# Per-layer gate: all four pairs' weight sums made by transfers, e's first half read back behind the pairs

## The chip, the cores and the metric

The kernel runs on one core of a Trainium2 chip. The metric is the device time of one execution in microseconds (us). The core's engines are TensorE (PE, with its weight loads PEld), VectorE (DVE), ScalarE (ACT), GpSimd (POOL) and SyncE (SP). Here SP issues nearly all transfers, and POOL issues only the transfers that add to what they find.

## The reference

One decoder layer over 256 tokens of width 2048: a mixer of two attention branches, a feed-forward part with a causal convolution, and a per-layer embedding with a gate. The change is in the last part, of which this is the whole:

```python
h = h + rmsnorm(f, g_ffn_post[i])
e = p[i] @ w_ple_in[i]                       # (256, 256) @ (256, 2048)
h = h + jax.nn.sigmoid((h @ w_ple_gate[i]).astype(jnp.float32)).astype(h.dtype) * e
```

All is float32. `w_ple_gate` is 2048 x 2048, so `h @ w_ple_gate` has 16 blocks of 128 along the sum (k) and 16 columns of 128.

## The kernel before

**Items.** All weights lie packed in one tensor `w`, in the order in which PE uses them, as items of 128 x 1024 floats (eight 128 x 128 blocks). An item is loaded into a tile `raw` (a ring of NRAW = 5), by `load` on SP. ScalarE copies it to `hi` in a rounded format (function `high`, L238, or L234 for sums), and VectorE subtracts to get the rest, `lo` (function `low`, L301, or L295 for sums). `hi` and `lo` are rings of NSPL = 7. A product is three matmuls (`three_wide`, L945): hi by hi, lo by hi, hi by lo. `lows` makes the `lo` of items up to a number, and then issues the raw loads for which a `raw` tile has come free. `tick` is called at each new item: it first calls deferred ScalarE jobs, then `high` for the items ahead, `lows`, and deferred VectorE jobs. Every engine works its instructions in the order in which this code writes them.

**Gate stage.** It has 40 items. Items 0 to 7 are columns 0 to 3 (two k blocks in each; loop over `k`, 16 steps). Items 8 to 13 are k = 8 to 13 of columns 4 to 11, eight blocks each. Items 14 to 29 are four "pairs" of k blocks, (0,1), (2,3), (4,5), (6,7), of the same columns, which are multiplied by a Strassen scheme (`strassen`): it needs seven products (21 matmuls) instead of eight. Items 30 and 31 are k = 14 and 15, and items 32 to 39 are columns 12 to 15 (`four`): t = 0 and t = 1 are the two halves of the tokens, and from k = 10 on t = 0 is finished first, then t = 1, the end of it in two parts.

**Pairs.** Each pair has four items: two raw ones with weights (14, 18, 22, 26 full; 17, 21, 25, 29 of which half is split) and between them two items of sums of weights. `weight_sums` makes them on VectorE: the first item by two additions (L254, L255), the second from the first by two more (L257, L258). For pairs in `by_dma` the first item is made by transfers instead: `sum_to` (L271) loads one summand with a plain transfer on SP, and `add_to_sums` (L277) has POOL issue two transfers with `accum_op=OP.add` that add the other summand, and then L254 and L255 fall away and the second raw item of the pair is loaded by half. `DSUM` says for how many pairs: five in each quarter of the feed-forward part, two in the gate. `sum_early` issues them ahead, into tiles that are free there (`tsum`).

The other factor of a pair, sums of columns of `h`, is made by `parts`: four small additions on VectorE, a copy on ScalarE, a subtraction on VectorE into `mixed` (L1209 to L1218). The list `made[n]` holds these three steps of mixture n.

**e.** Half of e (columns 0 to 1023) is computed early, and written to a tensor `e0` in HBM. The other half is computed at the start of the gate stage and kept in the tile `ee` (128 x 2 x 2048: t, columns), columns 1024 to 2047 of each t. Its first half is read back in two transfers inside the loop over k (L1559, at n = 5 and 6, where n = k // 2 + 1 at odd k).

**End.** `finish` multiplies the gate by `ee`, adds `hx` (h) and writes out. Column 0 to 511 of both t's come first, then 512 to 1535 of each t after a sigmoid, then 1536 to 2047, t = 1 in two halves.

Of the kernel before, what the change touches and what calls it, by code (L numbers as in the profile page):

```python
# [8 lines left out]
F32 = mybir.dt.float32  # L9
# [6 lines left out]
D = 2048  # L16
KT = D // 128
# [16 lines left out]

PAIRS = 4
DROWS = 10
DSUM = {"down": DROWS // 2, "pg": 2}
SETTLE = dict(even=8, turned=9)

TURNED = {("qk", s, 1): 3 for s in (2, 3)}  # L40
# [100 lines left out]
def hybrid_block_kernel(ctx: ExitStack, tc: tile.TileContext, head, gx, pT, convp, bias, masks, gains, w, out):  # L141
    nc = tc.nc
# [11 lines left out]
    def scope(name, **kw):  # L154
        st = ExitStack()
        return st, st.enter_context(tc.tile_pool(name=name, bufs=1, reuse_waits="tile", **kw))
# [6 lines left out]
    for g in _plan():  # L163
        if g[0] == "pad":
            short.append(used // 8)
        if _pairs(g):
# [4 lines left out]
            for p in range(_pairs(g)):  # L171
                i, r = len(stream), len(stream) - 2 * len(sums_of)
                stream += [r, None, None, r + 1]
                sums_of[i] = i + 3
                if g[0][0] == "pairs" and p < DSUM[g[0][1]]:
                    early_sums.append(i)
# [51 lines left out]
    def high(i, a=0, b=1024, src=None):  # L228
        if i not in hi:
            hi[i] = wsp.tile([128, 1024], F32R, name="hi")  # L230
            lo[i] = wsp.tile([128, 1024], F32R, name="lo")
        if i in sums:
            for n, x in enumerate(weight_sums(i)):
                ACT.activation(hi[i][:, n * 512:(n + 1) * 512], x, AF.Copy)  # L234
            return
        if i in part:
            b = 512
        ACT.activation(hi[i][:, a:b], raw[i][:, a:b] if src is None else src, AF.Copy)  # L238
# [30 lines left out]
    def sum_to(i, to):  # L269

        nc.sync.dma_start(to, w[stream[i] - NE])  # L271
        add_to_sums(i, [to[:, :512], to[:, 512:]])

    def add_to_sums(i, to):

        for x in to:
            nc.gpsimd.dma_start(x, w[stream[i] + 1 - NE][:, 512:], accum_op=OP.add)  # L277
        raw[i + 1] = to

    def sum_early(n):  # L280

        i = early_sums.pop(0)
        if n != 1:
            sum_to(i, mps["mp"].tile([128, 1024], F32, name="tsum", tag=f"hx{n - 1}" if n else "tsum"))
            return
        to = [tmp.tile([128, 512], F32, name="tsum", tag="t", bufs=2) for _ in range(2)]
        for c, x in enumerate(to):
            nc.sync.dma_start(x, w[stream[i] - NE][:, c * 512:(c + 1) * 512])
        add_to_sums(i, to)
# [13 lines left out]
    waiting, jobs, mps = [], [], {}  # L303

    def defer(*stages):


        waiting.append(list(stages))
# [8 lines left out]
    def lows(upto):  # L317

        while at["low"] < min(upto, at["cap"]):
            low(at["low"])  # L320
            at["low"] += 1
        while at["load"] in place and at["load"] < gone[at["low"]] + NRAW:
            load(place[at["load"]])
            at["load"] += 1

    def tick(i):


        now = due()
        for act, _ in now:  # L330
            act and act()
        before = at["high"]
        upto = -1 if at["hold"] else reach(i)
        at["look"] = min(at["look"] + at["grow"], NSPL - 1)
        while at["high"] <= upto:
            high(at["high"])
            at["high"] += 1
        late = len(waiting) > 2
        for _, dve in now:
            late and dve and dve()  # L340
        if not at["hold"]:
            lows(max(before, min(i + 2, at["high"])))
        for _, dve in now:
            late or dve and dve()
# [9 lines left out]
    def block(n=1):  # L354

        b = at["block"]
        at["block"] = b + n
        i, c = divmod(b, 8)
        if c == 0:
            tick(i)  # L360
        return hi[i][:, c * 128:(c + n) * 128], lo[i][:, c * 128:(c + n) * 128]
# [642 lines left out]
    for j in range(0, KT, 4):  # L1004
        if j:
            ga, gb = gate_groups(j, merged)
        else:
            for kind in ("ga", "gb"):
# [3 lines left out]
                if kind == "ga":  # L1012
# [7 lines left out]
                    mg_sc, mp = scope("mp")  # L1020
# [81 lines left out]
    def cut(src, k, t):  # L1102
        return [src[:, k, i * T + t * H:i * T + (t + 1) * H] for i in range(2)]
# [73 lines left out]
    def residual():  # L1177
        return [fp.tile([128, 2, 512], F32, name="hx", tag=f"hx{n}") for n in range(4)]

    hx = residual()  # L1180
# [5 lines left out]
    e0 = dram.tile([128, 2, D // 2], F32, name="e0")  # L1186
# [11 lines left out]
    def mixing(ps):  # L1198
        x = keep.tile([128, PAIRS, 2, 4, H], F32R, name="mixed", tag="gh")
        for p in range(ps):  # L1200
            mixed[p] = x[:, p] if p < PAIRS else fp.tile([128, 2, 4, H], F32R, name="mixed4", tag="hx0")
# [108 lines left out]
    def join(o, bk):  # L1310

        tt = DVE.tensor_tensor
        tt(o[1, 0], bk[7], o[0, 1], OP.add)
        tt(o[1, 1], bk[5], o[1, 0], OP.subtract)
        tt(o[0, 1], bk[5], o[0, 1], OP.subtract)
# [74 lines left out]
    def weigh(t, n):  # L1390
        o = ff[:, t, n * 512:(n + 1) * 512]
        DVE.tensor_tensor(o, o, g3[:, n * 512:(n + 1) * 512], OP.mult)
# [7 lines left out]
    for q in range(NQ):  # L1400
# [35 lines left out]
        def reload(n):  # L1436
            nc.sync.dma_start(hx[n], h1[:, :, n * 512:(n + 1) * 512])
# [25 lines left out]
        if end:  # L1463
            hx = residual()
# [14 lines left out]
    def apply(a, b, ts=range(2)):  # L1479

        for t in ts:
            x = hx[a // 512][:, t, a % 512:a % 512 + b - a]
            DVE.scalar_tensor_tensor(x, ff[:, t, a:b], rs[:, t], x, op0=OP.mult, op1=OP.add)
# [4 lines left out]
    for t in range(2):  # L1488
        to = ff[:, t, 3 * 512:]
# [10 lines left out]
    ee = fp.tile([128, 2 * D + 3 * 512], F32, name="ee", tag="ft")  # L1500
    xs = [ee[:, 2 * D + n * 512:2 * D + (n + 1) * 512] for n in range(3)]
    xs.append(fp.tile([128, 512], F32, name="xs", tag="cpad"))
    ee = ee[:, :2 * D].rearrange("p (t c) -> p t c", t=2)
# [3 lines left out]
    def turn_back(n):  # L1507
        turned[n] = bank()
        for k in range(2):
            for t in range(2):  # L1510
                a = (2 * n + k) % 4 * 128
                PE.transpose(turned[n][:, k * T + t * H:k * T + (t + 1) * H], hx[n // 2][:, t, a:a + 128], idf)

    def high3(n):
        x, to = turned[n].rearrange("p (a b) -> p a b", a=2), u3[:, 2 * n:2 * n + 2]
        ACT.activation(to[:, :, :T], x, AF.Copy)

    def save3(n):
        n < PAIRS and ACT.activation(xs[n], turned[n], AF.Copy)

    def low3(n):
        x, to = turned[n].rearrange("p (a b) -> p a b", a=2), u3[:, 2 * n:2 * n + 2]
        DVE.tensor_tensor(to[:, :, T:], x, f(to[:, :, :T]), OP.subtract)  # L1523

    def mixture(n):
        return parts(n, xs[n][:, :T], xs[n][:, T:])

    def ahead():
        lows(at["high"])
        high(at["high"])  # L1530
        at["high"] += 1
# [8 lines left out]
    def keep_e(n):  # L1540
        c, t = divmod(n, 2)
        ACT.activation(ee[:, t, D // 2 + c * 512:D // 2 + (c + 1) * 512], pse[n], AF.Copy)
# [8 lines left out]
    made = []  # L1551
    for k in range(KT):
        if k % 2 and k < KT - 1:
            n = k // 2 + 1
            turn_back(n)
            high3(n)
            low3(n)
            n == 1 and reload(3)
            n in (5, 6) and nc.sync.dma_start(ee[:, :, (n - 5) * 512:(n - 4) * 512], e0[:, :, (n - 5) * 512:(n - 4) * 512])  # L1559
            save3(n)  # L1560
            n < 4 and keep_e(n)
            n < 7 and apply(256 * n + 256, 256 * n + 512)
            n < 3 and [weigh(t, n + 1) for t in range(2)]
            n == 6 and [stage() for stage in made[0][1:]]
            if n == KT // 2 - 1:
                made.append(mixture(1))
                [stage() for stage in made[1]]
            n <= DSUM["pg"] and sum_early(n - 1)
        if k == 8:
            mixing(PAIRS)  # L1570
        if k == 10:
            made.append(mixture(0))
            made[0][0]()
        if k % 2 and k < KT - 2:
            ahead()
        w2 = block(4)
        for t in range(2):
            three_wide(ps[t], cut(u3, k, t), w2, k == 0, k == KT - 1)
    at["hold"], at["look"], at["grow"] = False, 2, 1
    ACT.preload_act_table(AF.Sigmoid)  # L1580
    def finish(spans):

        for t, a, b in spans:
            o = ff[:, t, a:b]
            DVE.tensor_tensor(o, o, ee[:, t, a:b], OP.mult)
            for c in range(a, b, 512):
                x = min(b - c, 512)
                to = ff[:, t, c:c + x]
                DVE.tensor_tensor(to, to, hx[c // 512][:, t, c % 512:c % 512 + x], OP.add)
            nc.sync.dma_start(out[:, t, a:b], o)  # L1590
# [12 lines left out]
    bk = next(s)  # L1603
    join_first(o, bk)
    defer((None, lambda bk=bk, o=o: join(o, bk)))
    next(s)
    defer((None, lambda bk=bk, o=o: ends(o, bk)))
    defer((None, lambda: finish([(t, 0, 512) for t in range(2)])))
    for t in range(2):
        defer((lambda t=t: ACT.activation(ff[:, t, 512:1536], ff[:, t, 512:1536], AF.Sigmoid),  # L1610
               lambda t=t: finish([(t, 512, 1536)])))
    ps = [bank() for _ in range(2)]
    four(("pg", 12), ps, u3, by=6, split=4)
    flush()
# [78 lines left out]
```

## Time and profile before

| | us |
|---|---|
| median of 3 executions | 1428.39 (1427.77 to 1428.44) |
| the profiled execution, its time | 1427.80 |
| the profiled execution, its span | 1426.0 |
| TensorE busy | 1418.9 |
| VectorE busy | 1174.4 |
| ScalarE busy | 866.9 |
| gate stage in the span | about 1329 to the end |

Times in views are microseconds from the span's start. A line of a timeline gives the start, the length, the engine, the line of the kernel, the instruction, what it writes and reads with the shapes, and how many are merged; in brackets the idle time of the engine before it and what ended that. SPq and POOLq are the queues that issue transfers. A matmul's length overlaps the next one's, so the distance between starts is its cost. The granted clock of TensorE was 0.999.

### The profile page before, as it was taken

Reading aid. Unit: us, or ns where it says so; the run is one execution under the profiler, and the core shown is the slowest. Engines: PE = TensorE matmul, PEld = TensorE weight load, DVE = VectorE, ACT = ScalarE, POOL = GpSimd, SP = SyncE. Lnnn points to the kernel's source line nnn. Section 1 sums busy time; section 2 is a strip of 40 time slices with the busy share of each in tenths; the row PEclk is TensorE's granted clock in tenths of the full one; section 3 lists DMA queues with packets and bytes.
Section 4 is the critical chain, followed back from the end, with each engine's and each line's share of the span. In section 5 each row is a group of like instructions: output and inputs, shape, how many; then the busy total and the mean of one; then the engine's idle time right before and its main releaser. Section 6 shows DMA issues by size and latency. Waiting matters only on the chain.

```text
span 1426.0 us, 20698 instructions
## 1 busy us (share of the span) xinstructions
PE 1418.9 (100%) x7499; PEld 1219.8 (86%) x7499; DVE 1174.4 (82%) x1821; ACT 866.9 (61%) x1316; POOL 60.5 (4%) x73
## 2 busy tenths in 40 slices
PE   9999999999999999999999999999999999999998
PEld 8888888888888888898888888888888888888886
DVE  7876666569889865689999788997889978899798
ACT  7665555566655655576666656655566555666564
POOL 0000000002110000000000000000000000000000
PEclk9999999999999999999999999999999999999999
DMA  7754746469986766648876886377873778628754
GB/s 293 268 165 156 248 146 222 150 237 250 303 229 201 264 219 215 201 168 265 256 204 209 266 265 213 103 262 237 267 214 100 263 236 267 214 99 289 247 186 163
DMA packets 95959, 312.26 MB, mean 219 GB/s; under 512 B 10480, under 2 KB 11120, under 8 KB 95728
## 3 DMA queue, kind: packets, MB, share of 16 engines
q1 hardware_dynamic: 86064, 293.10, 60.6%
q0 software_dynamic: 9792, 17.83, 7.4%
q8 instruction: 59, 0.97, 0.3%
q14 instruction: 44, 0.36, 0.1%
HBM read 305.64 MB, written 5.24 MB: 218 GB/s over the span
## 4 chain that ended last, share of the span: by engine, by line
PE 98%; DVE 2%; ACT 0%; issue 0%; ACTq 0%
PE mm L382 33%; PE mm L945 29%; PE mm L384 17%; PE mm L708 2%; PE mm L710 2%; PE mm L709 2%; PE mm L863 2%; PE mm L864 2%; PE mm L865 2%; PE S L382 0%; DVE lo L301 0%; PE mm L404 0%; PE mm L403 0%; PE mm L402 0%; PE S L721 0%; PE po L721 0%
## 5 line engine op out<-in xcount | busy, mean ns | idle before, releaser
L301 DVE TENSOR_TENSOR lo<-raw,hi 128x1024 fp32r<-128x1024 f32 (+1 forms) x498 | 579.1, 1180 | 96.1 <-ACT hi L238 91.4
L382 PE MATMUL mm<-u,hi 128*128 128x512 f32 x1804 | 627.8, 392 | 0.0
L238 ACT ACTIVATE hi<-raw 128x1024 fp32r<-128x1024 f32 (+1 forms) x498 | 502.1, 1022 | 173.3 <-PE mm L382 54.5
L384 PE MATMUL mm<-u,lo 128*128 128x256 f32 x1791 | 501.5, 280 | 0.0
L382 PEld LDWEIGHTS mm<-u,hi 128*128 128x128 f32 x1804 | 336.7, 187 | 72.7
L384 PEld LDWEIGHTS mm<-u,lo 128*128 128x128 f32 x1791 | 338.5, 189 | 0.7
L945 PE MATMUL mm<-hi,ft 128*128 128x512 f32 x504 | 162.6, 389 | 0.0
L945 PE MATMUL mm<-hi,u 128*128 128x512 f32 (+1 forms) x464 | 147.9, 389 | 0.2
L440 ACT ACTIVATE t<-mm 128x256 f32<-128x256 f32 x131 | 49.7, 380 | 149.3 <-PE mm L384 149.3
L945 PEld LDWEIGHTS mm<-hi,ft 128*128 128x128 f32 x504 | 94.6, 188 | 20.0 <-DVE ff L1308 0.4
L945 PEld LDWEIGHTS mm<-hi,u 128*128 128x128 f32 x464 | 86.4, 188 | 18.5 <-DVE u L1523 0.9
L945 PE MATMUL mm<-lo,ft 128*128 128x512 f32 x252 | 98.5, 391 | 0.0
L443 DVE TENSOR_TENSOR s<-mm,t 128x256 f32<-128x256 f32 x116 | 48.9, 422 | 51.9 <-ACT t L440 51.9
L945 PE MATMUL mm<-lo,u 128*128 128x512 f32 (+1 forms) x232 | 89.8, 387 | 0.8 <-DVE lo L301 0.6
L382 PE MATMUL mm<-mg,hi 128*128 128x512 f32 x232 | 80.5, 392 | 0.0
L277 POOL DMA_DIRECT2D tsum<-in_w x44 | 38.8, 1022 | 881.2 <-DMA tsum<-in_w 309.7
L234 ACT ACTIVATE hi<-wsum 128x512 fp32r<-128x512 f32 x76 | 46.2, 629 | 42.6 <-DVE wsum L257 30.2
L945 PE MATMUL mm<-hi,mixed 128*128 128x512 f32 x192 | 67.0, 389 | 0.0
L384 PE MATMUL mm<-mg,lo 128*128 128x256 f32 x230 | 64.4, 280 | 0.0
L1232 ACT ACTIVATE cv<-cpad,cw 128x256 f32<-128x256 f32 x88 | 52.5, 596 | 12.0 <-DVE cpad L1227 11.9
L945 PEld LDWEIGHTS mm<-lo,ft 128*128 128x128 f32 x252 | 47.3, 188 | 10.6 <-DVE lo L295 1.1
L945 PEld LDWEIGHTS mm<-lo,u 128*128 128x128 f32 x232 | 43.6, 188 | 10.2 <-DVE lo L301 1.2
(327 smaller groups left out, 1913.8 us busy)
## 6 DMA issues: line engine op xcount, KB each, us to landing
raw<-in_w SPq DMA_DIRECT2D x466, 512.0 KB, 4.3
tsum<-in_w POOLq DMA_DIRECT2D x44, 256.0 KB, 7.1
raw<-in_w SPq DMA_DIRECT2D x36, 256.0 KB, 2.9
tsum<-in_w SPq DMA_DIRECT2D x17, 512.0 KB, 4.4
gh<-in_w SPq DMA_DIRECT2D x12, 512.0 KB, 5.5
gh<-in_w POOLq DMA_DIRECT2D x24, 256.0 KB, 7.4
hd<-in_head SPq DMA_DIRECT2D x6, 576.0 KB, 7.3
gh<-in_gx SPq DMA_DIRECT2D x6, 512.0 KB, 4.4
```

What stands on the lines that cost most here:

```text
L234: ACT.activation(hi[i][:, n * 512:(n + 1) * 512], x, AF.Copy)
L238: ACT.activation(hi[i][:, a:b], raw[i][:, a:b] if src is None else src, AF.Copy)
L277: nc.gpsimd.dma_start(x, w[stream[i] + 1 - NE][:, 512:], accum_op=OP.add)
L301: DVE.tensor_tensor(lo[i][:, a:b], raw[i][:, a:b] if src is None else src, f(hi[i][:, a:b]), OP.subtract)
L382: PE.matmul(ps, wh, rhs, start=first, stop=last, skip_group_check=True)
L384: PE.matmul(ps[:, :T], wl, rhs[:, :T], start=False, stop=last, skip_group_check=True)
L440: ACT.activation(t1[0], ps[:, T:], AF.Copy)
L443: DVE.tensor_tensor(out, ps[:, :T], t1[0], OP.add)
L708: PE.matmul(pv[t], xh, wh, start=kt == 0, stop=False)
L709: PE.matmul(pv[t], xh, wl, start=False, stop=False)
L945: PE.matmul(ps, x[i], w[j], start=first and n == 0, stop=last and n == 2, skip_group_check=True)
L1232: ACT.activation(y, c[:, 2:], AF.Identity, scale=cw[:, n, 2:3], bias=cw[:, n, 3:4])
```

## The change

`DSUM["pg"]` goes from 2 to 4, so that the first item of sums of pairs three and four is also made by transfers. Their place is the first half of `ee` (128 x 1024 for each of t = 0 and 1), at n = 4 and 5 of the loop. The readback of e's first half leaves the loop and is issued, one transfer for each t, after the first part of the Strassen product, behind all raw loads. `mixture(1)` is split: its four additions stay, its copy and subtraction come after `ahead()`, the next item's `lo` and `hi`. At the end `finish` for columns 0 to 511 is done for each t for itself, beside the sigmoids.

```diff
-DSUM = {"down": DROWS // 2, "pg": 2}
+DSUM = {"down": DROWS // 2, "pg": PAIRS}
...
-    def sum_early(n):
+    def sum_early(n, to=None):
 
         i = early_sums.pop(0)
+        if to is not None:
+            sum_to(i, to)
+        elif n != 1:
+            sum_to(i, mps["mp"].tile([128, 1024], F32, name="tsum", tag=f"hx{n - 1}" if n else "tsum"))
         if n != 1:
-            sum_to(i, mps["mp"].tile([128, 1024], F32, name="tsum", tag=f"hx{n - 1}" if n else "tsum"))
             return
...
-            n in (5, 6) and nc.sync.dma_start(ee[:, :, (n - 5) * 512:(n - 4) * 512], e0[:, :, (n - 5) * 512:(n - 4) * 512])
...
                 made.append(mixture(1))
-                [stage() for stage in made[1]]
-            n <= DSUM["pg"] and sum_early(n - 1)
+                made[1][0]()
+            n <= 2 and sum_early(n - 1)
+            n in (4, 5) and sum_early(n - 2, ee[:, n - 4, :D // 2])
...
         if k % 2 and k < KT - 2:
             ahead()
+        k == KT - 3 and [stage() for stage in made[1][1:]]
...
     defer((None, lambda bk=bk, o=o: join(o, bk)))
+    for t in range(2):
+        nc.sync.dma_start(ee[:, t, :D // 2], e0[:, t])
     next(s)
     defer((None, lambda bk=bk, o=o: ends(o, bk)))
-    defer((None, lambda: finish([(t, 0, 512) for t in range(2)])))
     for t in range(2):
         defer((lambda t=t: ACT.activation(ff[:, t, 512:1536], ff[:, t, 512:1536], AF.Sigmoid),
-               lambda t=t: finish([(t, 512, 1536)])))
+               lambda t=t: finish([(t, 0, 512)])))
+        defer((None, lambda t=t: finish([(t, 512, 1536)])))
```

PE's instructions are the same, in the same order. In the changed kernel line numbers behind `sum_early` are 3 to 6 higher.

VectorE at the end of items 0 to 7, where mixture 1 is made (`y` are its four additions, `mixed` its subtraction, `lo<-raw,hi` the items' rest). Before:

```order
L1210 TENSOR_TENSOR y_13357<-y_13357,ee 128x128
L1211 TENSOR_TENSOR y_13357<-ee 128x128
L1212 TENSOR_TENSOR y_13357<-y_13357,ee 128x128
L1218 TENSOR_TENSOR mixed<-y_13357,mixed 128x512
L301 TENSOR_TENSOR lo<-raw,hi 128x1024 x3
```

After:

```order
L1213 TENSOR_TENSOR y_13361<-y_13361,ee 128x128
L1214 TENSOR_TENSOR y_13361<-ee 128x128
L1215 TENSOR_TENSOR y_13361<-y_13361,ee 128x128
L304 TENSOR_TENSOR lo<-raw,hi 128x1024
L1221 TENSOR_TENSOR mixed<-y_13361,mixed 128x512
L304 TENSOR_TENSOR lo<-raw,hi 128x1024 x2
```

The `lo` of item 8 has moved ahead of `mixed`; those of items 9 and 10 stay behind it.

VectorE in pair three (pair four reads the same), from the second raw item of pair two on. Before:

```order
L301 TENSOR_TENSOR lo<-raw,hi 128x512
L254 TENSOR_TENSOR wsum<-raw 128x512
L255 TENSOR_TENSOR wsum<-raw 128x512
L301 TENSOR_TENSOR lo<-raw,hi 128x1024
L295 TENSOR_TENSOR lo<-wsum,hi 128x512 x2
L257 TENSOR_TENSOR wsum<-wsum,raw 128x512
L258 TENSOR_TENSOR wsum<-wsum,raw 128x512
L295 TENSOR_TENSOR lo<-wsum,hi 128x512 x2
```

After:

```order
L304 TENSOR_TENSOR lo<-raw,hi 128x512
L304 TENSOR_TENSOR lo<-raw,hi 128x1024
L257 TENSOR_TENSOR wsum<-ee,raw 128x512
L258 TENSOR_TENSOR wsum<-wsum,raw 128x512
L298 TENSOR_TENSOR lo<-ee,hi 128x512 x2
L298 TENSOR_TENSOR lo<-wsum,hi 128x512 x2
```

L254 and L255 are gone, and the additions of the second item (L257, L258) now stand ahead of the `lo` of the first, which reads `ee`.

VectorE at the end, from the last four additions of the Strassen part on (L1338 before, L1341 after; `lo` are items 37 to 39, `ff<-ff,ee` the product of `finish`). Before:

```order
L1338 TENSOR_TENSOR ff<-ff,mm 128x512 x4
L301 TENSOR_TENSOR lo<-raw,hi 128x1024 x2
L1585 TENSOR_TENSOR ff<-ff,ee 128x512
L1589 TENSOR_TENSOR ff<-ff,hx 128x512
L1585 TENSOR_TENSOR ff<-ff,ee 128x512
L1589 TENSOR_TENSOR ff<-ff,hx 128x512
L301 TENSOR_TENSOR lo<-raw,hi 128x1024
L1585 TENSOR_TENSOR ff<-ff,ee 128x1024
```

After:

```order
L1341 TENSOR_TENSOR ff<-ff,mm 128x512 x4
L304 TENSOR_TENSOR lo<-raw,hi 128x1024
L1589 TENSOR_TENSOR ff<-ff,ee 128x512
L1593 TENSOR_TENSOR ff<-ff,hx 128x512
L304 TENSOR_TENSOR lo<-raw,hi 128x1024 x2
L1589 TENSOR_TENSOR ff<-ff,ee 128x1024
```

The first product with `ee` now stands ahead of the `lo` of items 38 and 39, and the second one's t = 1 behind them. On SP the two transfers into `ee` now stand behind the last raw load and ahead of the first output; on ScalarE the first of the two sigmoids stands ahead of the `hi` of item 39.

## Prediction

> **What bounds the kernel now.** I read the page first, for the engine whose work is the end, and then the waits of that engine alone.
>
> ```profile
> span 1426.0 us, 20698 instructions
> PE 1418.9 (100%) x7499; PEld 1219.8 (86%) x7499; DVE 1174.4 (82%) x1821; ACT 866.9 (61%) x1316; POOL 60.5 (4%) x73
> ...
> PE 98%; DVE 2%; ACT 0%; issue 0%; ACTq 0%
> ```
>
> ```profile
> PE z L594 <- DVE epsb L563: 1.1, 1, 1.1
> PE mm L945 <- DVE lo L301: 0.6, 1, 0.6
> PE mm L945 <- DVE lo L295: 0.2, 1, 0.2
> ```
>
> TensorE is the bound: 98% of the chain is matmuls, and in the whole span PE waited three times by the table of waits. The first wait is the start. The other two, 0.6 and 0.2 us, both lie in the gate stage that is changed, and both wait for a `lo` written by VectorE. The change leaves PE's instructions alone, in kind and order, so it can give back only what PE loses in those places, and can take away only by making a new wait. The table counts too little, since a matmul also loses time while its weights wait, so I read PE's timeline by the distance from start to start (columns: start, us, instruction, in brackets the idle time before it).
>
> ```profile
> 1340.36 0.43 PE L945 MATMUL mm<-lo,u 128*128 128x512 f32 x1
> 1340.90 0.73 PE L945 MATMUL mm<-hi,u 128*128 128x512 f32 x2
> ...
> 1355.39 0.61 PE L945 MATMUL mm<-hi,u 128*128 128x512 f32 x2
> 1355.84 0.39 PE L945 MATMUL mm<-lo,u 128*128 128x512 f32 x1
> 1356.07 0.61 PE L945 MATMUL mm<-hi,u 128*128 128x512 f32 x2
> 1357.26 0.50 PE L945 MATMUL mm<-lo,u 128*128 128x512 f32 x1 [0.57 <-DVE lo L301]
> 1357.59 0.63 PE L945 MATMUL mm<-hi,u 128*128 128x512 f32 x2
> ...
> 1390.03 0.39 PE L945 MATMUL mm<-lo,mixed 128*128 128x512 f32 x1
> 1390.26 0.39 PE L945 MATMUL mm<-hi,mixed 128*128 128x512 f32 x1
> 1390.77 0.49 PE L945 MATMUL mm<-hi,u 128*128 128x512 f32 x1
> 1391.50 0.50 PE L945 MATMUL mm<-lo,u 128*128 128x512 f32 x1 [0.23 <-DVE lo L295]
> 1391.83 0.39 PE L945 MATMUL mm<-hi,u 128*128 128x512 f32 x1
> ```
>
> In stride a matmul follows the last by 0.23 us (1390.03 to 1390.26), and two of them by 0.45 (1355.39 to 1355.84). Stall A: after 1356.07 the next but one was due at 1356.52 and came at 1357.26, 0.74 late; the one behind it lost 0.10 more (0.33 for 0.23). A is 0.84 us. Stall B: 0.51, 0.73 and 0.33 us in place of 0.23, so 0.28 + 0.50 + 0.10 = 0.88 us. A third loss, at 1340.90 (0.54 for 0.23, 0.31 us, and about 0.1 in the next), waits for a `u` that the change does not touch. Whose lateness makes A and B is seen on DVE.
>
> ```profile
> 1350.59 1.04 ACT L238 ACTIVATE hi<-raw 128x1024 fp32r<-128x1024 f32 x1
> ...
> 1354.39 0.28 DVE L1212 TENSOR_TENSOR y<-y,ee 128x128 f32<-128x128 f32 x1
> 1355.38 0.69 DVE L1218 TENSOR_TENSOR mixed<-y,mixed 128x512 fp32r<-128x512 f32 x1 [0.70 <-ACT mixed L1215]
> 1355.98 2.35 DVE L301 TENSOR_TENSOR lo<-raw,hi 128x1024 fp32r<-128x1024 f32 x2
> 1359.67 1.23 DVE L301 TENSOR_TENSOR lo<-raw,hi 128x1024 fp32r<-128x1024 f32 x1 [1.33 <-ACT hi L238]
> ...
> 1378.24 0.68 DVE L254 TENSOR_TENSOR wsum<-raw 128x512 f32<-128x512 f32 x1
> 1378.84 0.68 DVE L255 TENSOR_TENSOR wsum<-raw 128x512 f32<-128x512 f32 x1
> 1379.44 1.21 DVE L301 TENSOR_TENSOR lo<-raw,hi 128x1024 fp32r<-128x1024 f32 x1
> ...
> 1385.10 0.68 DVE L254 TENSOR_TENSOR wsum<-raw 128x512 f32<-128x512 f32 x1
> ```
>
> ```profile
> 1357.00:1374.00 17.00, 16.74 (x74) 13.87 (x75) 15.56 (x26) 12.40 (x18) 0.00 (x0) 1.00 0.61 190
> 1374.00:1391.00 17.00, 16.87 (x75) 13.64 (x73) 16.79 (x26) 9.40 (x15) 0.00 (x0) 1.00 0.49 158
> ```
>
> A is the `lo` of item 8: DVE stood 0.70 us for ScalarE's `mixed`, then did its own `mixed`, and only then, at 1355.98, the `lo` that PE wanted. B is volume: in the second window (columns: length, PE, PEld, DVE, ACT, POOL) DVE is busy 16.79 of 17 us. From one pair's L254 at 1378.24 to the next one's at 1385.10 it takes 6.86 us, while the 21 matmuls of a pair take 21 x 0.227 = 4.8 (0.45 for two), so pairs three and four use up the lead.
>
> **The change, part by part.**
>
> Mixture 1's split behind the item's `lo`. The four small operations end at 1354.67, and item 8's `hi` has long been made (ScalarE's row at 1350.59), so the `lo` starts there, 1.3 us earlier, and ends at 1355.8, before 1356.52. A goes: -0.84. The split itself then runs inside what was idle time, ScalarE's copy under the `lo`; pair two wants it only after 1378. The next `lo` (item 9) ends about 1357.6 for a need at 1356.5 + 12 x 0.227 = 1359.2.
>
> Four additions fewer. Each of pairs three and four loses L254 and L255, 2 x 0.60 us by their starts, so DVE reaches the last pair's `lo` 2.4 us sooner. PE, 0.84 earlier by A, wants it 0.84 sooner than its stall-free time (1391.50 less 0.78), so at 1389.9; DVE has it at 1391.45 - 2.4 = 1389.0. B goes with 0.9 us to spare: -0.88. If ScalarE holds the pair instead, B stays whole; the nearest row for that is the 1.33 us at 1359.67, which comes before the pairs, so I take the full term.
>
> The transfers of the sums.
>
> ```profile
> 1340.31 6.12 SPq L204 DMA_DIRECT2D raw<-in_w  x3
> 1346.53 0.53 SPq L1559 DMA_DIRECT2D ee<-e  x1
> ...
> 1353.21 45.13 SPq L204 DMA_DIRECT2D raw<-in_w  x20
> ...
> L277 POOL DMA_DIRECT2D tsum<-in_w x4: 862/1052/1480, 1339.3 to 1344.0; - x4
> ...
> tsum<-in_w POOLq DMA_DIRECT2D x4, 256.0 KB, 8.0
> ee<-e SPq DMA_DIRECT2D x2, 512.0 KB, 7.7
> ```
>
> Two plain 512 KB transfers into `ee` stand where the two 512 KB readbacks stood, each one raw load earlier on SP. The raw loads there are let go by DVE's `lo`, not by SP, so they keep their times: the first sum is issued in the gap after the second raw load (estimate 1343.4), the second at about 1346.7. They land 7.7 us later, as the readbacks did, at 1351.1 and 1354.4. POOL then issues four accumulations (0.86 to 1.48 us each; it has nothing else), the last at about 1356.5, landed by 1364.5. DVE first reads these sums where L254 stood, 1378.24: 13 us of cover. The new bytes (4 x 256 KB, less 2 x 256 KB for halves of raw loads that fall away) come where the DMA share is 0.61, and no `hi` waited for a raw load there. Cost 0; from both sides, no gain, and a loss of at most about 1 us if a raw load slips by a slot.
>
> POOL's queue and a rule. The four issues of before took at most 1.48 us while DVE, 82% busy over the span, went on. The Trainium skill, page "SBUF — State Buffer", section "SBUF: two separate sides", says that a transfer issued from POOL cannot have its descriptors written while VectorE runs an operation in a mode that takes both its ports. That gives a result of its own and is a rival below; these four issues speak against it.
>
> The readback behind the pairs. SP issues it after the last raw load, 1398.3 in before's time, so at about 1398.9 and 1399.5; landed 7.7 us later, 1406.6 and 1407.2, and 1 to 2 us sooner as DVE frees the raw tiles sooner. Who stands behind it on DVE:
>
> ```profile
> 1405.55 2.35 DVE L301 TENSOR_TENSOR lo<-raw,hi 128x1024 fp32r<-128x1024 f32 x2
> 1407.82 0.68 DVE L1585 TENSOR_TENSOR ff<-ff,ee 128x512 f32<-128x512 f32 x1
> ...
> 1410.48 1.22 DVE L301 TENSOR_TENSOR lo<-raw,hi 128x1024 fp32r<-128x1024 f32 x1
> ...
> 1416.80 0.60 ACT L1594 ACTIVATE ff<-mm 128x512 f32<-128x512 f32 x1 [9.71 <-PE mm L945]
> 1421.03 0.66 ACT L1618 ACTIVATE ff<-mm 128x256 f32<-128x256 f32 x2 [3.63 <-PE mm L945]
> ```
>
> The product with `ee` for t=0 now stands before items 38 and 39. PE finishes t=0 at 1416.8 with 18 matmuls of items 37 to 39, so it wants 38 twelve matmuls earlier, at 1414.0, and 39 at 1415.3; 1.7 sooner with A and B gone: 1412.3 and 1413.6. If the readback lands at L, DVE has 38 at L + 1.3 + 1.2 and 39 at L + 3.7. L may be 1409.8 at no cost; I expect 1405 to 1406.6. Cost 0, with 3 us to spare. Splitting `finish` changes neither its bytes nor the last three spans, so the tail behind 1421.0 stays at 5 us. One sigmoid more ahead of the last `hi` is about 1 us on ScalarE, which then idled 9.71 us.
>
> Sum: -0.84 - 0.88 = -1.72 us on the profiled execution: span 1424.3, time 1427.8 - 1.7 = 1426.1 (1.8 us lie around the span). That execution is 0.6 below the median of 1428.39, so the median comes to 1426.7.
>
> **The rivals.**
>
> Only A goes: ScalarE's `hi` of the last pair, or a raw load, takes the place of DVE's volume. For it: in the chain ScalarE's `hi` stands between DVE's sum and its `lo` of that pair. Against: `lo` of the transferred sums now lies between them. 1428.39 - 0.84 = 1427.6.
>
> Nothing: both waits come back elsewhere, or the slipped load costs about what A gives. 1428.4.
>
> Slower, by the readback: DVE stands at the product with `ee`, items 38 and 39 behind it, and PE waits. It decides from a landing at 1409.8; each us more costs one. To end slower by 0.2% it must land at 1409.8 + 1.7 + 2.9 = 1414.4, 15.5 us after its issue, where the two of before took 7.7. At 1414.4 the time is 1431.3.
>
> Slower, by POOL being shut out: DVE is nearly never free from 1359.67, so accumulations not issued by then are issued only when DVE itself stands at the sum for pair three, near 1378. With 1.5 us of issue and 8.0 of landing the sum is there at 1387.5 and its `lo` some 2 us later, at 1389.5. PE comes to that sum 6 matmuls into pair three; pair four's thirteenth was due at 1390.49, so pair three's seventh at 1390.49 - 27 x 0.227 = 1384.4, and 1383.5 without A. That is 6 us lost, about 1433. The rule named above would do this.
>
> Faster by over 0.2% is out of reach of the stage: with the loss at 1340.90 gone too it is 0.84 + 0.88 + 0.41 = 2.1 us, 1426.3, less than the 2.9 that 0.2% is.
>
> **How the numbers follow.** Both stalls go: 0.71, 1426.7, own range 1426.1 to 1427.2. Only one goes: 0.14. Nothing, or a small loss: 0.10. Readback late enough for 0.2%: 0.02. POOL shut out: 0.01. Something better that I don't see: 0.02. 0.2% is about what a measurement of this kernel can tell from no change, so the first three are all "the same": 0.95, faster 0.02, slower 0.03. The range goes from 1426.3 less the 0.7 that the three runs of before are apart (1425.6) up to no change and 0.3 more (1428.7).
>
> **What would show it.** PE's timeline without the idle time at the end of the first gate group and without the two gaps at the last pair's `hi,u` and `lo,u`; L257 reading `ee` in pairs three and four and no L254 there; POOL's four rows into `ee` near 1351 to 1357; the two readbacks landed before DVE's first product with `ee`, or DVE idle there by under 3 us. I am wrong if PE waits for a `lo` in the last group, or for a sum of pair three or four.

## The result, and the profile after

The changed kernel takes 1426.19 us (median of 22 runs, 1425.62 to 1428.69), the kernel before 1428.14 (22 runs beside them, 1427.30 to 1430.38). The ratio is 0.9986, with a 95% interval of 0.998 to 0.9993: about 2 us faster, less than 0.2%. The profiled execution took 1426.48 us.

The page, with PE's busy time, and the chain:

```profile
span 1424.7 us, 20711 instructions
PE 1418.5 (100%) x7499; PEld 1219.9 (86%) x7499; DVE 1171.9 (82%) x1817; ACT 866.8 (61%) x1316; POOL 64.0 (4%) x77
...
PE 98%; DVE 0%; DMA 0%; ACT 0%; SPq 0%; issue 0%
```

DVE has left the chain (2% to 0%), as the four additions (1817 instructions for 1821) and the two waits went. PE's waits now have one row, the start of the kernel:

```profile
PE z L597 <- DVE epsb L566: 1.1, 1, 1.1
```

PE's timeline in the three places (start, us, instruction):

```profile
1341.01 0.44 PE L948 MATMUL mm<-lo,u 128*128 128x512 f32 x1
1341.56 0.73 PE L948 MATMUL mm<-hi,u 128*128 128x512 f32 x2
1342.13 0.40 PE L948 MATMUL mm<-lo,u 128*128 128x512 f32 x1
...
1356.03 0.61 PE L948 MATMUL mm<-hi,u 128*128 128x512 f32 x2
1356.49 0.39 PE L948 MATMUL mm<-lo,u 128*128 128x512 f32 x1
...
1390.26 0.39 PE L948 MATMUL mm<-hi,u 128*128 128x512 f32 x1
1390.49 0.39 PE L948 MATMUL mm<-lo,u 128*128 128x512 f32 x1
1390.71 0.39 PE L948 MATMUL mm<-hi,u 128*128 128x512 f32 x1
```

Where stall A was, the distances are 0.46 and less; where B was, 0.23 and 0.22. Only the third loss stands, 0.55 for 0.23 at 1341.56 and 0.57 for 0.45 behind it. From the stage's first matmul (of the product for e's second half, 1324.59 before and 1325.25 after) to the end of the last, PE took 96.40 us before and takes 94.57: 1.83 less. "Stage" below is this length, and comparisons between profiles are made by times from the stage's start.

VectorE at the five places that matter, and then ScalarE at two:

```profile
1355.26 1.22 DVE L304 TENSOR_TENSOR lo<-raw,hi 128x1024 fp32r<-128x1024 f32 x1
1356.39 0.69 DVE L1221 TENSOR_TENSOR mixed<-y,mixed 128x512 fp32r<-128x512 f32 x1
...
1365.80 0.69 DVE L257 TENSOR_TENSOR wsum<-tsum,raw 128x512 f32<-128x512 f32 x1 [0.45 <-DMA raw<-in_w]
1367.70 0.69 DVE L258 TENSOR_TENSOR wsum<-wsum,raw 128x512 f32<-128x512 f32 x1 [1.21 <-DMA raw<-in_w]
...
1386.28 0.68 DVE L257 TENSOR_TENSOR wsum<-ee,raw 128x512 f32<-128x512 f32 x1
...
1388.81 1.28 DVE L298 TENSOR_TENSOR lo<-wsum,hi 128x512 fp32r<-128x512 f32 x2
...
1405.14 0.69 DVE L1589 TENSOR_TENSOR ff<-ff,ee 128x512 f32<-128x512 f32 x1
...
1421.52 0.43 DVE L1593 TENSOR_TENSOR ff<-ff,hx 128x256 f32<-128x256 f32 x1
...
1363.22 1.07 ACT L238 ACTIVATE hi<-raw 128x1024 fp32r<-128x1024 f32 x1 [1.02 <-DMA raw<-in_w]
1365.79 1.06 ACT L238 ACTIVATE hi<-raw 128x1024 fp32r<-128x1024 f32 x1 [1.50 <-DMA raw<-in_w]
```

Item 8's `lo` starts right behind the four small additions and ahead of `mixed`. The sum of pair four reads `ee`. The product with `ee` for t = 0 starts at 1405.14 with no wait. New are two waits of VectorE for raw loads at the sums of pair one, 0.45 + 1.21 = 1.66 us, and two of ScalarE's `hi`, 1.02 + 1.50 = 2.52 us; the kernel before has none of these. In the stretch where the DMA share was 0.61 it is now 0.86 (columns: length, PE, PEld, DVE, ACT, POOL, clock, DMA share, GB/s).

```profile
1357.00:1374.00 17.00, 17.00 (x77) 14.08 (x76) 14.10 (x24) 12.11 (x18) 1.65 (x2) 1.00 0.86 245
```

PE does not feel the waits: the `lo` of the last pair ends at 1390.09 and PE uses it at 1390.49, 0.40 us to spare.

### The profile page after: what moved, and what is told of

Same layout as the page of the kernel before. It is cut to its first block, busy times and chain, and to the rows that moved or that the text cites. A ratio compares the mean times of both kernels' runs of the same rounds, so it can differ in the third digit from the quotient of the medians.

```text
span 1424.7 us, 20711 instructions
## 1 busy us (share of the span) xinstructions
PE 1418.5 (100%) x7499; PEld 1219.9 (86%) x7499; DVE 1171.9 (82%) x1817; ACT 866.8 (61%) x1316; POOL 64.0 (4%) x77
## 4 chain that ended last, share of the span: by engine, by line
PE 98%; DVE 0%; DMA 0%; ACT 0%; SPq 0%; issue 0%
PE mm L385 33%; PE mm L948 31%; PE mm L387 17%; PE mm L713 2%; PE mm L711 2%; PE mm L712 2%; PE mm L867 2%; PE mm L866 2%; PE mm L868 2%; PE S L385 0%; PE mm L407 0%; PE mm L406 0%; PE mm L405 0%; DMA hd<-in_head 0%; PE S L724 0%; PE po L724 0%
## 5 line engine op out<-in xcount | busy, mean ns | idle before, releaser
L385 PEld LDWEIGHTS mm<-mg,hi 128*128 128x128 f32 x232 | 43.3, 187 | 9.3
```

The lines of the kernel that those rows point to most:

```text
L385: PE.matmul(ps, wh, rhs, start=first, stop=last, skip_group_check=True)
```

## The experiments

Each run stands beside runs of the kernel before, whose medians were 1428.05 to 1428.16.

| kernel | median, us | ratio (95%) | stage, us | PE's losses in the stage, us |
|---|---|---|---|---|
| before | 1428.14 | | 96.40 | third 0.42, A 0.84, B 0.89 |
| changed | 1426.19 | 0.9986 (0.998 to 0.9993) | 94.57 | third 0.43 |
| split of mixture 1 alone | 1427.10 | 0.9992 (0.9984 to 1.0001) | 95.42 | third 0.43, B 0.80 |
| transfers alone | 1427.04 | 0.9992 (0.9983 to 1.0001) | 95.49 | third 0.45, A 0.83 |
| pair three's sums alone | 1426.61 | 0.9988 (0.9979 to 0.9996) | 94.60 | third 0.45 |
| sums issued later | 1426.09 | 0.9987 (0.9978 to 0.9995) | 94.58 | third 0.45 |
| no additions for pair four | 1426.38 | 0.9988 (0.9979 to 0.9997) | 94.57 | third 0.43 |
| overwriting for pair four | 1426.39 | 0.9989 (0.9979 to 0.9999) | 94.61 | third 0.42 |
| readback twice | 1426.28 | 0.9988 (0.9979 to 0.9997) | 94.57 | third 0.42 |
| readback three times | 1429.00 | 1.0008 (0.9999 to 1.0017) | 94.84 | third 0.4, new 0.25 at 1412 |
| products at n = 4 | 1426.73 | 0.999 (0.9981 to 0.9999) | 94.79 | new 0.48 and 0.27 |
| the same with pair three alone | 1426.44 | 0.9989 (0.998 to 0.9998) | 94.83 | new 0.49 and 0.27 |
| products spread | 1425.87 | 0.9985 (0.9976 to 0.9994) | 94.12 | none |
| the same with pair three alone | 1425.77 | 0.9984 (0.9976 to 0.9993) | 94.12 | none |

The losses are sums of distances between starts, good to about 0.02 us. Six kernels of the table lose the third loss alone, and their stages lie within 0.04 us (94.57 to 94.61), where the intervals of their ratios are 1.9 to 2.9 us wide; so the verdicts on the stalls rest on the stages, one profile for each kernel.

**Each half alone.** From the kernel before, with only the split of mixture 1:

```diff
-                [stage() for stage in made[1]]
+                made[1][0]()
...
+        k == KT - 3 and [stage() for stage in made[1][1:]]
```

> The kernel before with one edit: mixture 1's copy and subtraction behind the next item's lo; sums of pairs three and four stay on VectorE. Theory (stalls A and B are terms of their own, and VectorE comes to the pairs about 1 us sooner too): the idle time of 0.57 at item 8 is gone, the gaps in pair four stay at 0.3 to 0.9 us, time 0.6 to 1.1 us under before, about 1427.2. Rival (VectorE's volume sets when pair four is served, whatever PE gained ahead of it): A's 0.84 comes back as a longer stall in pair four, 1.7 us there, and the time is that of before, 1428.1.

PE at the last pair, then VectorE's `lo` for it:

```profile
1388.91 0.39 PE L945 MATMUL mm<-hi,mixed 128*128 128x512 f32 x1
1389.32 0.50 PE L945 MATMUL mm<-hi,u 128*128 128x512 f32 x1
1390.04 0.51 PE L945 MATMUL mm<-lo,u 128*128 128x512 f32 x1 [0.23 <-DVE lo L295]
1390.39 0.39 PE L945 MATMUL mm<-hi,u 128*128 128x512 f32 x1
...
1388.65 1.34 DVE L295 TENSOR_TENSOR lo<-wsum,hi 128x512 fp32r<-128x512 f32 x2
```

The theory held. A is gone and B stands, 0.18 + 0.49 + 0.12. The stage is 0.98 shorter. PE came about 1 us sooner and yet B did not grow, since VectorE came sooner too: that `lo` starts 64.55 us behind the stage's start (1324.10), where before it was 65.52.

From the changed kernel, with the split taken back:

```diff
-                made[1][0]()
+                [stage() for stage in made[1]]
...
-        k == KT - 3 and [stage() for stage in made[1][1:]]
```

> The changed kernel with mixture 1's three steps in one place again, ahead of item 8's lo. Theory: stall A is back in full, 0.74 + 0.10 us at item 8, and pair four has no gap, since PE reaches it 0.84 us later: time 0.8 us over the changed kernel, about 1427.0. Rival (the sums on transfers are what frees VectorE, and its order at item 8 no longer matters): no idle time at item 8, time as the changed kernel, 1426.2.

```profile
1355.85 0.62 PE L948 MATMUL mm<-hi,u 128*128 128x512 f32 x2
1357.02 0.50 PE L948 MATMUL mm<-lo,u 128*128 128x512 f32 x1 [0.55 <-DVE lo L304]
1357.36 0.64 PE L948 MATMUL mm<-hi,u 128*128 128x512 f32 x2
...
1387.20 1.29 DVE L298 TENSOR_TENSOR lo<-wsum,hi 128x512 fp32r<-128x512 f32 x2
```

The theory held again. PE's timeline has A as before (1.17 for 0.45, and 0.34) and no B. The stage is 0.91 shorter. The halves add up: 0.98 + 0.91 = 1.89 for 1.83 together. The last row is VectorE's `lo` for the last pair: it starts 62.84 us behind the stage's start (1324.36), 2.68 sooner than before, and ends 2.03 us ahead of PE (1388.49 for 1390.52). VectorE waits for no raw load here, although all four adding transfers are there.

**Half the transfers.**

```diff
-DSUM = {"down": DROWS // 2, "pg": PAIRS}
+DSUM = {"down": DROWS // 2, "pg": 3}
...
-            n in (4, 5) and sum_early(n - 2, ee[:, n - 4, :D // 2])
+            n == 4 and sum_early(n - 2, ee[:, n - 4, :D // 2])
```

> The changed kernel with the sums of pair three alone on transfers (1 x 512 KB and 2 x 256 KB fewer early; pair four's L254 and L255 are back on VectorE). In the changed kernel VectorE had the last pair's lo at 1390.06, 0.43 us before PE used it. Theory (stall B is VectorE's volume): 1.2 us more of it, so a stall of 0.5 to 0.9 us in pair four, time 1426.7 to 1427.1. Rival (what helps is that lo of the transferred sums lies between, or the waits for raw loads that the four adding transfers bring eat half): with two adding transfers fewer VectorE waits about 0.8 us less for raw loads and no gap shows in pair four, time 1426.2.

VectorE's `lo` of the last pair and PE's first use of it:

```profile
1389.64 1.34 DVE L298 TENSOR_TENSOR lo<-wsum,hi 128x512 fp32r<-128x512 f32 x2
...
1391.75 0.39 PE L948 MATMUL mm<-lo,u 128*128 128x512 f32 x1
```

The rival held: B is gone with half the dose, and the lead is larger, 0.77 us for 0.40. (The profiled execution lost 1.0 us elsewhere, so the stage counts, not the span.) VectorE waits for no raw load here. So in the changed kernel pair four's transfers take 1.2 us of additions off VectorE and give back 1.66 us of waits. The next three runs ask why.

**What the transfers cost the loads beside them.** First their time was moved:

```diff
-            n in (4, 5) and sum_early(n - 2, ee[:, n - 4, :D // 2])
+            n in (6, 7) and sum_early(n - 4, ee[:, n - 6, :D // 2])
```

> The changed kernel with the sums of pairs three and four issued at n = 6 and 7 of the loop over k in place of 4 and 5, some 6 us later. In the changed kernel VectorE waited 0.45 and 1.21 us for raw loads at L257 and L258 of pair one (1365 to 1368) and ScalarE 1.0 and 1.5 us, which the kernel before did not. Theory (the four adding transfers, which ran from 1354 to 1368, slow the raw loads of that time): the waits for raw loads move about 6 us later, to items 17 to 22 (1366 to 1375), with 1 to 2 us on VectorE in all; the sums land by 1374, ahead of their use at 1378.8, and the time stays within 0.5 us of 1426.2. Rival (those waits come from the raw loads having been put behind a plain 512 KB transfer each on SP): they stay at 1362 to 1368 with the plain transfers' new place, or vanish, and none is seen at 1368 to 1375.

POOL's issues moved by 1 to 3 us only (the last from 1360.31 to 1362.15), and VectorE still waited 1.26 us for a raw load at 1366.66. The move is too small to tell anything of the cause. Then POOL's additions for pair four were left out:

```diff
+    last_pair = [early_sums[-1]]
...
-        for x in to:
+        for x in to if i != last_pair[0] else ():
```

> The changed kernel without POOL's two adding transfers for pair four; the plain transfer stays, so that pair's sums lack one summand. Raw loads issued between 1350 and 1366 landed in a median of 4.0 us before, 4.8 with pair three alone on transfers, 6.6 in the changed kernel. Theory (the adding transfers are what slows the raw loads): 4.6 to 5.2 us here, no wait of VectorE for a raw load at L257 and L258 of pair one (0.45 and 1.21 us in the changed kernel) or under 0.4 in all, and the last pair's lo 1 us or more ahead of PE in place of 0.4. Rival (the plain transfers on SP ahead of each raw load do it): 6 us or more, VectorE waits 1 us or more. Time 1426.2 by both, as PE has no gap there either way.

The theory held. Raw loads landed in a median of 5.2 us, VectorE's waits are gone, and the last pair's `lo` ends 2.09 us ahead of PE (1387.82 for 1389.91), 1.69 more than in the changed kernel, which had lost 1.66. The other runs say the same: the six kernels of the table that have both the split and four adding transfers made VectorE wait 0.94 to 1.72 us for raw loads, and the five with two adding transfers not at all. But four adding transfers are not enough by themselves, since without the split there was no wait: VectorE came to the first of these sums 0.85 us later there (40.95 us behind the stage's start for 40.10), and the load had landed. Whether the waits come from the bytes of the two transfers or from the adding, the last run asked, in which they overwrite:

```diff
+            if i != last_pair[0]:
                 nc.gpsimd.dma_start(x, w[stream[i] + 1 - NE][:, 512:], accum_op=OP.add)
+            else:
+                nc.gpsimd.dma_start(x, w[stream[i] + 1 - NE][:, 512:])
```

> The changed kernel, but POOL's two transfers for pair four's sums overwrite what they find instead of adding to it (this pair's sums then hold the second summand alone). Same bytes to load, same queue, same number of transfers. Theory that the adding itself is what delays the loads beside it: with two adding transfers left the 512 KB raw loads issued between 1350 and 1366 land in a median 4.8 to 5.6 us, as with pair four's adding transfers left out (5.2) or with pair three's alone (4.8), the DMA share in 1357 to 1374 is at most 0.72, and VectorE waits under 0.4 us for raw loads at the sums of pair two. Rival, that it is the bytes and the queue: 6.0 to 7.4 us, a share of 0.8 or more, and a wait of 1 us or more, as in the changed kernel (6.6; 0.86; 1.66). The time is 1425.7 to 1426.6 by both, since pair four's lo is in time either way.

The theory missed on one of its three numbers: raw loads issued between 1350 and 1366 landed in 7.0 us, not 4.8 to 5.6. The other two held: a DMA share of 0.66 and no wait of VectorE for a raw load, at pair one's sums or at pair two's. The DMA queues from 1354 to 1370 (packets, MB, share of 16 engines; q0 is POOL's), for the changed kernel, for overwriting, and without these two transfers:

```profile
q1 hardware_dynamic: 1082, 3.38, 55.7%
q0 software_dynamic: 576, 1.05, 38.3%
```

```profile
q0 software_dynamic: 443, 1.04, 26.7%
```

```profile
q0 software_dynamic: 288, 0.52, 18.3%
```

Adding 1.05 MB took 38.3% of the stretch in packet time, 36.5% for a MB. Overwriting took 26.7 - 18.3 = 8.4% for 0.52 MB, 16.2% for a MB (if pair three's adding took the same in both runs), as the raw loads do (55.7 / 3.38 = 16.5%). So the packets of an adding transfer take 2.2 times as long as those of a plain one of the same bytes. Most of that is their number: 288 packets for 0.52 MB with adding, 443 - 288 = 155 with overwriting, and one packet took 0.16 and 0.14 us. (Packets are the pieces in which the engines move data.) Packets overlap, as the share passes 1, so these are times under load.

The raw loads that pair one's sums wait for are the two issued between 1358 and 1362, 512 and 256 KB (items 14 and 17). The columns are their times to landing and the waits for raw loads between 1352 and 1374, all in us:

| kernel | 512 KB | 256 KB | ScalarE waits | VectorE waits |
|---|---|---|---|---|
| before | 4.4 | 2.9 | 0 | 0 |
| no additions for pair four | 5.7 | 4.0 | 0.8 | 0 |
| overwriting for pair four | 6.6 | 5.0 | 2.1 | 0 |
| changed | 7.4 | 7.0 | 2.5 | 1.66 |
| transfers alone | 6.2 | 5.3 | 1.1 | 0 |

The bytes alone slow these loads (overwriting against no additions), and in the changed kernel adding slows them more. Up to 1362 the DMA engines are full either way, with a share of 1.0. Behind 1362 the share is 0.80 for overwriting and 1.07 for adding up to 1366, then 0.36 and 0.69 up to 1370; in the changed kernel the later of the two loads lands at 1367.70. That the adding itself, and not the time at which it was issued, makes VectorE wait is likely but not shown: overwriting's transfers were issued from 1351.74 to 1355.3, the adding ones one by one up to 1360.31. In the run with spread products (further below) the four adding ones began at 1352.00, and the waits were 1.22 + 0.50 us all the same, but their last was issued at 1359.68. And the last row has the adding of the changed kernel with landings near those of overwriting.

**How late the readback may be.** It is issued two or three times over, each behind the last, so that the last lands later:

```diff
-    for t in range(2):
+    for t in (0, 1) * 3:
         nc.sync.dma_start(ee[:, t, :D // 2], e0[:, t])
```

> The changed kernel with the readback of e's first half made three times in a row (t = 0, 1, 0, 1, 0, 1), each behind the one before of the same t; the product with e waits for the last. In the changed kernel t = 0 landed at 1404.2 and VectorE never waited. PE wants items 38 and 39 at about 1412.9 and 1414.3 there, so a landing up to 1410.4 should be free, and each us more should cost one. Theory: two more rounds of 6 to 7 us, landing of t = 0 near 1417, time 5 to 8 us over the changed kernel, by landing less 1410.4. Rival (PE has a cover that I don't see, or the rounds overlap): landing near 1408 or a stall under 1 us, time within 1 us of the changed kernel.

> The changed kernel with the readback of e's first half made twice in a row (three times in late_back, where t = 0 landed at 1409.3 and the time was 1429.0). In late_back's profile VectorE worked without a break from that landing to its end, 12.8 us, and ended 3.1 us behind the last matmul, where it ends 1.9 us behind it in the changed kernel. Theory (VectorE's own queue behind the product with e decides, from a landing of about 1409 in the changed kernel's time, not PE's need of items 38 and 39): one more round lands near 1406, VectorE waits 1 to 2 us, and the time stays 1426.2 within 0.4. Rival (any wait there costs): time over by what VectorE waits, 1427.2 or more.

VectorE, and PE where item 38's `lo` is needed, with three:

```profile
1409.29 0.69 DVE L1589 TENSOR_TENSOR ff<-ff,ee 128x512 f32<-128x512 f32 x1 [6.14 <-DMA ee<-e]
...
1421.72 0.42 DVE L1593 TENSOR_TENSOR ff<-ff,hx 128x256 f32<-128x256 f32 x1
...
1411.31 0.61 PE L948 MATMUL mm<-hi,u 128*128 128x512 f32 x2
1411.90 0.50 PE L948 MATMUL mm<-lo,u 128*128 128x512 f32 x1
1412.23 0.63 PE L948 MATMUL mm<-hi,u 128*128 128x512 f32 x2
```

And VectorE with two:

```profile
1406.32 0.69 DVE L1589 TENSOR_TENSOR ff<-ff,ee 128x512 f32<-128x512 f32 x1 [2.19 <-DMA ee<-e]
```

Two copies make VectorE wait 2.19 us, a little over the 1 to 2 expected, and cost nothing (stage 94.57), as the theory had it. With three, neither theory nor rival held: the product started at 1409.29, where a landing near 1417 was expected, and the median was 2.8 us over the changed kernel's. PE loses 0.14 + 0.11 us at item 38, and the larger loss is VectorE's own: from the product at 1409.29 to its end at 1422.14 it never waits again, 12.85 us of work. In the changed kernel the same work ends at 1421.95 with 1.16 + 2.60 us of waits for ScalarE in it; so a landing costs from 1421.95 - 12.85 = 1409.1 on, in that execution's time. Counted from the stage's start, that is a landing at 83.85 us. The two runs lie on either side of it: with two copies the product starts at 82.23 and VectorE ends where it ends in the changed kernel (96.69 for 96.70), with three it starts at 85.21 and VectorE ends 1.36 later. That profiled execution, 1426.95 us, was the fastest of 11 (up to 1431.4); no profile shows where the others lost more. A still later landing is one possible cause.

**The third loss.** PE's third loss waits for the `u` at 1341, which comes late behind two products of 128 x 512 on VectorE (the step `weigh`, line 1395). In the changed kernel:

```profile
1338.48 1.28 DVE L1395 TENSOR_TENSOR ff<-ff,g 128x512 f32<-128x512 f32 x2
1339.69 1.22 DVE L304 TENSOR_TENSOR lo<-raw,hi 128x1024 fp32r<-128x1024 f32 x1
1340.82 0.68 DVE L1526 TENSOR_TENSOR u<-mm,u 128x512 fp32r<-128x512 f32 x1
```

First both were moved to n = 4, and the same was done with pair three's sums alone:

```diff
-            n < 3 and [weigh(t, n + 1) for t in range(2)]
+            n in (1, 4) and [weigh(t, 2 if n == 1 else 3) for t in range(2)]
```

> The changed kernel with the two products by g3 (weigh) of columns 1536 to 2047 moved from n = 2 to n = 4 of the loop over k. The one loss that PE has left in the stage, 0.32 and 0.11 us at 1341.7, follows VectorE's u for n = 3, ahead of which stood those two products (1.28 us) and an item's lo. Theory: u comes 0.4 us sooner or more, the gap goes, and the time is 0.4 us under the changed kernel, 1425.8. Rival (ScalarE's copy for that u, or the lo, holds it): the gap stays and the time is 1426.2.

> The kernel with the sums of pair three alone on transfers, with the same products moved as in weigh4. With pair three alone VectorE had the last pair's lo 0.7 us ahead of PE, with both pairs 0.4 us, since the second pair's adding transfers cost VectorE 1.66 us of waits for raw loads and saved 1.2. Theory: no gap on PE in the stage but those of the transpositions, 1425.8, as weigh4. Rival: the products at n = 4 push the lo of item 8 or of the pairs late, a gap of 0.3 us or more at item 8 or in pair four, 1426.2 or more.

```profile
1347.52 0.50 PE L948 MATMUL mm<-lo,u 128*128 128x512 f32 x1
1348.12 0.73 PE L948 MATMUL mm<-hi,u 128*128 128x512 f32 x2
...
1351.19 0.39 PE L948 MATMUL mm<-lo,u 128*128 128x512 f32 x1
1351.58 0.73 PE L948 MATMUL mm<-hi,u 128*128 128x512 f32 x2
```

Both theories missed: the loss moved with the products, 0.60 for 0.23 at 1348.12 and 0.39 at 1351.58, in PE's timeline of the first of the two, and it grew from 0.43 to 0.75. In both steps tried, n = 2 and n = 4, two products beside an item's `lo` made the next `u` late; at n = 1 two stand without an item's `lo`, and PE loses nothing. So one was done at n = 2 and one at n = 3:

```diff
-            n < 3 and [weigh(t, n + 1) for t in range(2)]
+            n == 1 and [weigh(t, 2) for t in range(2)]
+            n in (2, 3) and weigh(n - 2, 3)
```

> The changed kernel with the two products by g3 of columns 1536 to 2047 spread: one at n = 2, one at n = 3 (before: both at n = 2; in weigh4 both at n = 4, where PE's gap of 0.43 us went from 1341.7 to 1348.1 and 1351.6 and grew to 0.75). A step of n lasts 3.2 us on PE, and VectorE has 2.5 us there with an item's lo and 3.7 with two products beside it. Theory: with one of 0.6 us it fits, the gap goes, the stage is 0.43 us shorter and the time 1425.8. Rival (any product beside a lo is too much): a gap of 0.2 us or more at n = 3 or 4, time 1426.2 or more.

> As ws, with the sums of pair three alone on transfers. Theory: no gap of PE in the stage but at the transpositions, the last pair's lo 0.7 us or more ahead of PE, time 1425.8, equal to ws. Rival: the spread products move pair four's lo late by 0.3 us or more, time 1426.2.

VectorE in the first of them:

```profile
1338.64 0.68 DVE L1395 TENSOR_TENSOR ff<-ff,g 128x512 f32<-128x512 f32 x1
1339.24 1.22 DVE L304 TENSOR_TENSOR lo<-raw,hi 128x1024 fp32r<-128x1024 f32 x1
1340.52 0.69 DVE L1526 TENSOR_TENSOR u<-mm,u 128x512 fp32r<-128x512 f32 x1
```

Both theories held. PE's stage has no gap left over 0.1 us and takes 94.12 us, 0.45 under the changed kernel's. Against the kernel before that is 2.28 us. The medians, 1425.87 and 1425.77, are the lowest of all, but their intervals overlap the changed kernel's, so a gain over it is shown by the profiles alone. With pair three alone the last pair's `lo` leads by 0.71 us (1388.98 for 1389.69), with both by 0.34.

## Why the prediction was right, point by point

**The bound and the two stalls.** Right. PE lost time by A and B, and both went. The terms were 0.84 + 0.88 = 1.72; the stage gave 1.83, and alone 0.98 and 0.91. Some 0.1 us of that lies in no gap that I read. The median was put at 1426.7 and came to 1426.19; about half of that difference is the base, 1428.39 from 3 runs and 1428.14 from 22. The rival in which only A goes did not come about, and its price was near: 1427.6, and 1427.10 with the split alone.

**B's spare time.** Put at 0.9 us, measured at 0.40, and by two errors against each other. The step "DVE reaches the last pair's `lo` 2.4 us sooner" was near for the transfers alone, 2.68, but left out what A frees on the same queue: the split alone brings that `lo` 0.97 us sooner. The two add up to 3.65, and without pair four's adding transfers it is 65.52 - 61.86 = 3.66 us sooner (1386.53, from the stage's start at 1324.67). In the changed kernel the gain was 65.52 - 63.56 = 1.96, as VectorE's waits took 1.66. These waits are the other error: the step "no `hi` waited for a raw load there. Cost 0" failed, since raw loads slipped, `hi` waited 2.52 us, and VectorE more than the 1 us allowed. The cost in time was 0 all the same, partly by luck: the forecast did not know of these waits, and 0.40 us of spare time was left. Half the dose would have been enough. The step took a free DMA share of 0.39 as room for half a MB more, but the packets of adding took 2.2 times as long as plain ones of the same bytes.

**The landing of the plain sums.** Taken as 7.7 us, from the readbacks; the two took a median 9.5. POOL's adding transfers began at 1354.46 and the last at 1360.31, where 1356.5 was forecast:

```profile
1354.46 1.76 POOL L277 DMA_DIRECT2D ee<-in_w  x2 [10.32 <-DVE u L1526]
1356.91 0.86 POOL L277 DMA_DIRECT2D ee<-in_w  x1 [0.69 <-DMA ee<-in_w]
1360.31 0.88 POOL L277 DMA_DIRECT2D ee<-in_w  x1 [2.54 <-issue]
...
1397.07 1.13 SPq L1611 DMA_DIRECT2D ee<-e  x2
```

The last took 7.4 us to land, so the sums were there by about 1368. They are first read at 1378.78, by ScalarE: 11 us of the forecast's 13 us of cover were left.

**The rival of POOL shut out.** It did not happen: these issues took 0.86 to 1.23 us each, while VectorE was busy 14.10 of 17 us. By the Trainium skill, page "SBUF — State Buffer", section "SBUF: two separate sides", VectorE in a mode with two ports would have kept POOL from writing descriptors. Nothing of that size is seen here beside VectorE's float32 operations, and no run here shows whether any of them uses such a mode.

**The readback.** Right that it hides: issued at 1397.07 (the last row above), it took a median of 7.3 us to landing, so it was there at about 1404.4, a little ahead of the forecast's 1405 to 1406.6, and the product came at 1405.14 without a wait. The rival's turning point was mis-sized. It went by PE's need of items 38 and 39, "L may be 1409.8", which in this execution's time, its stage 0.66 later, is 1410.5. VectorE's own work behind the product decides sooner, at 1409.1. The working asked who waits for what stands behind the product on VectorE's queue, but not whether that queue could still be emptied by the end. PE's need stood near where it was put: in the run with three copies the product started at the time of 1410.46 here, and PE lost 0.25 us at item 38.

**Out of reach.** With the third loss gone too, 2.1 us was worked out; the runs with spread products gave 2.28 in the stage.

## What to carry to other kernels

When a vector engine is nearly always busy ahead of the bound engine, a little work moved off it, or moved behind what the bound engine needs next, can remove the stall whole, and more than enough buys nothing: pair three's transfers did all that the two pairs' did. Price a transfer that adds by the time of its packets and by the loads that it delays, not by its bytes. For a transfer that moves towards the end, work out two limits for its landing, from the consumer of the queue behind it and from the work that the waiting engine must still finish, and take the earlier.

## What the runs showed of the hardware

The packets of transfers that add took 2.2 times as long for each byte as those of plain ones (36.5% and 16.2% of 16 us of all engines for a MB), mostly because there were more of them (288 and 155 for 0.52 MB). A 512 KB raw load beside them, issued between 1358 and 1362, took 7.4 us to land, 6.6 with overwriting in place of half of them, 4.4 in the kernel before. A plain 512 KB transfer took 9.5 us in a full stretch, 7.7 in the kernel before, and 7.3 at the end of the stage.
